# Attention scores of 64-channel heads: from two 128-row products per head to three 64-row products on the head's own half of the array

## The chip, the cores and the metric

The kernel runs on one core of one Trainium2 chip. A core has a matrix engine (TensorE, in the profile PE, with its loads of the stationary operand shown apart as PEld), a vector engine (VectorE, DVE), a scalar engine (ScalarE, ACT), a general engine (GpSimd, POOL) and a queue engine for transfers (SyncE, SP). Each engine takes its instructions in its own order and waits for the others by semaphores. The metric is the device time of one execution in microseconds (us).

A matrix product (MATMUL) multiplies a stationary operand, loaded beforehand by an LDWEIGHTS instruction, with a moving operand. Both lie in SBUF, with the contracted dimension along the 128 partitions, and the product is summed into a bank of PSUM. In a profile row `128*128 128x512` means 128 rows by 128 columns of stationary operand and a moving operand of 128 partitions by 512 elements.

## The reference

A two-layer encoder trunk on 512 tokens of 1024 channels, in float32. Layer 0 has an mLSTM mixer, layer 1 a banded attention; both have an attention to 256 memory tokens beside it, an output projection and a gated MLP with a causal convolution. What matters here are the two attentions with heads of 64 channels:

```python
def one_chunk(c):                      # band attention: 12 heads of 64 channels
    ...
    s = jnp.einsum('bqhd,bkhd->bhqk', qc, kc).astype(jnp.float32) * scale + bias
    s = jnp.where(valid, s, -jnp.inf)
    p = jax.nn.softmax(s, axis=-1).astype(vc.dtype)
    return jnp.einsum('bhqk,bkhd->bqhd', p, vc)

def memory_attention(q, mem, w_kv):    # 4 heads of 64 channels, in each of the two layers
    ...
    s = jnp.einsum('bshd,bmhd->bhsm', q, mk).astype(jnp.float32) * (MEM_HEAD_DIM ** -0.5)
    p = jax.nn.softmax(s, axis=-1).astype(mv.dtype)
    return jnp.einsum('bhsm,bmhd->bshd', p, mv).reshape(bsz, seq, MEM_WIDTH)
```

## The kernel before

All large products are done in a rounded float32 format (fp32r) with an operand cut in two: a high part, which is the value rounded to that format, and a low part, which is the rest. A product of two such numbers is summed from three products: high by high, high by low, low by high; the low by low term is left out. `mm3` (lines 194 to 196) issues these three for the projections, and nearly all rows of L194, L195 and L196 in the profile are such products.

Channels lie along the partitions, so a tile of 128 partitions holds a pair of heads: head 0 in partitions 0 to 63, head 1 in 64 to 127 (`HEADS`). For the scores of one head the kernel before uses the whole height of the array. `head_keys` makes for each head a tile whose own half holds the high part of the keys and whose other half holds their low part. `head_queries` makes two tiles for each head: one with the high part of the queries in both halves, one with the low part in the head's own half and zeros in the other (the zeros are a GpSimd memset, the copy into the other half an ACT instruction). `head_scores` (L600) then needs two products of 128 rows per head: the first gives high by high plus high by low, the second low by high. The four products of a pair stand head by head: both of head 0, then both of head 1.

Where these stand:

- `band_attention(j, ...)`, for six pairs j: `softmax(T)`, for four token tiles T of 128 tokens, calls `scores` with keys 0 to 128(T+1), so the moving operand is 128, 256, 384 and 512 wide. These are 24 calls. Six calls of `project_pair` make keys and queries.
- `memory_attention`, twice in each layer: four token tiles each against 256 memory tokens, 16 calls with a moving operand 256 wide. Four calls of `queries` and two of `load_memory_kv` make its operands.
- `mlstm_head` also calls `head_scores` (four heads, four tiles), and `qk_tile` calls `head_queries` and `head_keys` for it.

The order of the instructions on each engine comes from the order in which the program is written, which is woven: `weave` takes some steps of a filler (the projections of the next pair, or the output projection) for each step of the attention job, in the ratio that stands at the call, so that TensorE has products of the filler to do while the softmax of the attention runs on VectorE and ScalarE. A scheduler of the framework may move an instruction past others where its inputs come late; three PSUM banks (`psc`) are turned over by the scores, three by the projections (`pmm`), two by transposes and sums (`ptr`). The tiles of queries and keys come from a pool of 50 buffers of 128 x 512 (`u`).

Of the kernel before, what the change touches and what calls it, by code (L numbers as in the profile page):

```python
# [10 lines left out]
F32R = mybir.dt.float32r  # L11
I32 = mybir.dt.int32
AF = mybir.ActivationFunctionType
ALU = mybir.AluOpType
AX = mybir.AxisListType

P = 128
D = 1024
S = 512
# [7 lines left out]
HD = 64  # L27
# [22 lines left out]
def f(ap):  # L50
    return ap.bitcast(F32)
# [3 lines left out]
def trunk(  # L55
# [18 lines left out]
    nc = tc.nc  # L74
    V, A, G = nc.vector, nc.scalar, nc.gpsimd
# [14 lines left out]
    def sb(tag, shape, dtype=F32):  # L90
        count[0] += 1
        return pool.tile(shape, dtype, tag=tag, name=f"{tag}{count[0]}", bufs=bufs[tag])

    def ps(tag):
        count[0] += 1
        return psum.tile([P, S], F32, tag=tag, name=f"p{tag}{count[0]}", bufs=pbufs[tag])
# [38 lines left out]
    HEADS = (slice(0, HD), slice(HD, P))  # L135
# [3 lines left out]
    def split(hi, lo, src, on_act=True, pinned=False):  # L139
        high = A.copy(hi, src) if on_act else V.tensor_copy(hi, src)  # L140
        low = V.tensor_tensor(out=lo, in0=src, in1=f(hi), op=ALU.subtract)  # L141
        if pinned:
            pin(high)
            pin(low)
# [53 lines left out]
    def project(w, c0, act, tag="mm"):  # L198


        n = len(act)
        wh, wl = weights(rows(w, c0, P), n, P)
        o = ps(tag)
        for k in range(n):
            mm3(o, wh[:, k, :], wl[:, k, :], act[k][0], act[k][1], k == 0, k == n - 1)
            yield
        return o
# [250 lines left out]
    def value_weights(hf, u):  # L458
        n = AW // 2
        ex = rows(a_w_in, 4 * AW, 2 * AH, 2 * u, 2 * u + 2) if hf else None  # L460
        return load(rows(a_w_in, 2 * AW + hf * n, n, 2 * u, 2 * u + 2), 2, n, ex)

    with tc.manual_schedule(engines={mybir.EngineType.PE, mybir.EngineType.Activation, mybir.EngineType.DVE}):
# [56 lines left out]
        for q in range(KT // 2):  # L520
            k = 2 * q
# [39 lines left out]
        raw = value_weights(1, 0)  # L561
# [15 lines left out]
    def head_queries(t, scale=1.0):  # L577
        qs, ls = ([sb("u", [P, S], F32R) for _ in range(2)] for _ in range(2))
        for h, r in enumerate(HEADS):
            G.memset(f(ls[h])[HEADS[1 - h], :], 0.0)  # L580
            A.activation(qs[h][r, :], t[r, :], AF.Copy, scale=scale)
            V.scalar_tensor_tensor(ls[h][r, :], t[r, :], scale, f(qs[h])[r, :], op0=ALU.mult, op1=ALU.subtract)
        for h, r in enumerate(HEADS):
            A.copy(qs[h][HEADS[1 - h], :], f(qs[h])[r, :])
        return qs, ls

    def head_keys(t):
        ks = [sb("u", [P, S], F32R) for _ in range(2)]
        for h, r in enumerate(HEADS):
            A.copy(ks[h][r, :], t[r, :])  # L590
            V.tensor_tensor(out=ks[h][HEADS[1 - h], :], in0=t[r, :], in1=f(ks[h])[r, :], op=ALU.subtract)
        return ks

    def head_scores(o, h, q, tsl, k, c, first, keys_first=False):

        for i, part in enumerate(q):
            a, b = part[h][:, tsl], k[h][:, c]
            if keys_first:
                a, b = b, a
            nc.tensor.matmul(o, a, b, start=first and i == 0, stop=i == 1)  # L600

    def load_memory_kv(l):
        raw = sb("wr", [P, D])
        nc.sync.dma_start(raw, spill[l])
        k = head_keys(raw[:, :S])
        vs = []
        for m in range(2):
            v = sb("u", [P, S], F32R).rearrange("p (h c) -> p h c", h=4)
            src = raw[:, S + m * MEM : S + (m + 1) * MEM].rearrange("p (h c) -> p h c", h=4)
            split(v[:, :, :HD], v[:, :, HD:], src)  # L610
            vs.append(v)
        return k, vs
# [12 lines left out]
    def queries(o, row):  # L625

        if row is None:
            return head_queries(o, HD**-0.5)
        q = sb("t", [P, S])
        V.scalar_tensor_tensor(q, o, HD**-0.5, row, op0=ALU.mult, op1=ALU.mult)  # L630
        return head_queries(q)

    def scores(outs, q, tsl, k, c):

        for h in range(2):
            head_scores(outs[h], h, q, tsl, k, c, True)

    def memory_attention(q, kv, hp, mixes):

# [443 lines left out]
    e, u, c, r = (cpool.tile([P, TT, AH], F32, name=f"gate{i}") for i in range(4))  # L1083
# [131 lines left out]
    def mlstm_head(h):  # L1215
# [6 lines left out]
        def weighted_scores(s):  # L1222
            n = S - s * P
            sl = slice(s * P, (s + 1) * P)
            e = sb("t", [P, S])
            A.activation(e[:, :n], spreads.pop((h, s)), AF.Exp, bias=acol[:, s, h : h + 1])
            spread_exponents(order.index((h, s)) + NEXT)
            G.affine_select(
                out=e[:, :P], in_=e[:, :P], pattern=[[1, P]], base=0, channel_multiplier=-1,
                compare_op=ALU.is_ge, fill=0.0,  # L1230
            )
            yield
            o = ps("sc")
            kf, qf = ks[full], qs[full]
            mm3(o[:, :n], kf[0][:, sl], kf[1][:, sl], qf[0][:, s * P :], qf[1][:, s * P :], True, False)
            head_scores(o[:, :n], odd, qs[sh], slice(s * P, S), ks[sh], sl, False, True)
            V.scalar_tensor_tensor(e[:, :n], o[:, :n], DH**-0.5, e[:, :n], op0=ALU.mult, op1=ALU.mult)
            split(pt[:, RO[s] : RO[s + 1]], pt[:, 1280 + RO[s] : 1280 + RO[s + 1]], e[:, :n])
            yield
# [56 lines left out]
    run(fill)  # L1296
    fill = chain(a_tiles(2), a_memory_queries(0), a_tiles(3, 4), a_tiles(5), a_memory_queries(1))
    memkv = load_memory_kv(0)
    weave(mlstm_head(0), fill, 1.4)
    until(lambda: og[2] is not None, fill)  # L1300
# [38 lines left out]
    for j in range(KT):  # L1339
        wh, wl = weights(rows(ffn_w_down[0], j * P, P, FT - LAST, FT), LAST, P)  # L1340
        o = ps("mm")
# [23 lines left out]
    def project_pair(j):  # L1365
        def times_row(o):
            t = sb("t", [P, S])
            V.tensor_tensor(out=t, in0=o, in1=norm.row, op=ALU.mult)
            return t

        ov = yield from project(w_kv, AW + j * P, kvact)
        t = times_row(ov) if norm.row is not None else None
        o = yield from project(w_kv, j * P, kvact)
        if t is None:
            t = times_row(ov)
        k = head_keys(times_row(o))
        tp = ps("mm")
        for T in range(TT):
            nc.tensor.transpose(tp[:, T * P : (T + 1) * P], t[:, T * P : (T + 1) * P], ident)
        v = []  # L1380
        for i in range(2):

            w = sb("u" if j == 5 else ("fh", "fl")[i], [P, S], F32R).rearrange("p (h c) -> p h c", h=4)
            split(w[:, :, :HD], w[:, :, HD:], tp[:, i * MEM : (i + 1) * MEM].rearrange("p (h c) -> p h c", h=4))
            v += [w[:, :2, :], w[:, 2:, :]]
        q = queries((yield from project(b_w_in, j * P, act)), norm.row)
        qkv[j] = q, k, v
# [132 lines left out]
    for hf in range(2):  # L1520
# [6 lines left out]
        for Ts, pieces in groups:  # L1527
            for c in pieces:
                if c.start:
                    os_[Ts[0]] = ps("mm")  # L1530
                for u in range(n):
# [4 lines left out]
                    for T in Ts:  # L1536
                        for i in range(2):
                            k = 2 * u + i
# [58 lines left out]
```

## Time and profile before

| What | Value |
|---|---|
| median of 3 runs | 1179.24 us (1179.14 to 1179.31) |
| profiled execution, its own time | 1178.82 us |
| span of the profiled execution, first to last instruction | 1177.1 us |
| granted TensorE clock, mean | 0.999 |
| PE busy | 1167.3 us, 7005 products |
| DVE busy | 940.8 us |
| ACT busy | 728.9 us |
| POOL busy | 129.2 us |
| products of L600 (all score products of 64-channel heads, the mLSTM's 32 with them) | 192, busy 39.7 us together |

The busy time of PE counts the union of what its matmuls are shown to last, and these overlap: a 512-wide product is shown to last 0.39 us, while the next one starts 0.23 us after it. What a product costs on PE is therefore read from the distance between starts, in the view of instructions in order of time. The numbers after the bar in a group's row are busy us and mean ns of one; after the second bar stands the idle time of the engine just before them and what ended it.

### The profile page before, as it was taken

How to read it: one execution, taken by the hardware profiler on the slowest of the kernel's cores; microseconds unless marked ns; L12 is line 12 of the kernel's file. 1: busy time of each engine (PE TensorE's matmuls, PEld its weight loads, DVE VectorE, ACT ScalarE, POOL GpSimd, SP SyncE). 2: the span in 40 equal slices, each digit the busy share in tenths (PEclk: the TensorE clock that was granted, in tenths of full speed). 3: DMA queues.
4: the chain of work that ended last, by engine and by line, in shares of the span. 5: the costliest groups of instructions: out<-in, count | busy, mean ns of one | idle time of the engine just before them, and what ended most of it. 6: DMA issues, size and time to landing. Idle time of an engine off the chain costs nothing.

```text
span 1177.1 us, 18647 instructions
## 1 busy us (share of the span) xinstructions
PE 1167.3 (99%) x7005; PEld 1032.8 (88%) x7005; DVE 940.8 (80%) x1680; ACT 728.9 (62%) x1297; POOL 129.2 (11%) x222
## 2 busy tenths in 40 slices
PE   9999999999999999999999999999999999999997
PEld 9988888888889999999888888778889999999986
DVE  6777788887979878877688888897897887777755
ACT  6548677655656655666666677676565665666545
POOL 1111101010021121111020000101001011110100
PEclk9999999999999999999999999999999999999999
DMA  8645325243366766665563313325426466666551
GB/s 285 222 112 141 85 55 152 76 144 116 90 161 158 181 167 163 163 145 125 155 205 114 90 54 96 105 90 179 141 90 153 108 137 143 142 144 144 126 161 72
DMA packets 199420, 158.64 MB, mean 135 GB/s; under 512 B 8376, under 2 KB 178334, under 8 KB 199330
## 3 DMA queue, kind: packets, MB, share of 16 engines
q1 hardware_dynamic: 183170, 119.87, 34.6%
q0 software_dynamic: 15584, 36.67, 15.7%
q8 instruction: 55, 0.90, 0.3%
q10 hardware_dynamic: 576, 0.92, 0.2%
q14 instruction: 35, 0.29, 0.1%
HBM read 128.89 MB, written 32.46 MB: 137 GB/s over the span
## 4 chain that ended last, share of the span: by engine, by line
PE 95%; ACT 2%; DVE 2%; issue 0%; POOL 0%; POOLq 0%; DVEq 0%; ACTq 0%
PE pmm L194 18%; PE pmm L195 18%; PE pmm L196 18%; PE ptr L195 6%; PE ptr L194 6%; PE ptr L196 6%; PE psc L196 5%; PE psc L195 5%; PE psc L194 5%; PE psc L600 2%; PE ptr L1421 1%; PE ptr L1442 1%; PE ptr L1443 1%; PE ptr L669 0%; PE pmm L491 0%; PE pmm L470 0%
## 5 line engine op out<-in xcount | busy, mean ns | idle before, releaser
L194 PE MATMUL pmm<-u,wh 128*128 128x512 f32 (+1 forms) x968 | 333.2, 345 | 0.3 <-ACT u L140 0.3
L196 PE MATMUL pmm<-u,wl 128*128 128x512 f32 (+1 forms) x968 | 330.6, 342 | 0.0
L195 PE MATMUL pmm<-u,wh 128*128 128x512 f32 (+1 forms) x968 | 330.4, 341 | 0.0
L141 DVE TENSOR_TENSOR wl<-wr,wh 128x1024 fp32r<-128x1024 f32 (+3 forms) x172 | 199.7, 1162 | 83.0 <-ACT wh L140 81.5
L140 ACT CAST wh<-wr 128x1024 fp32r<-128x1024 f32 (+3 forms) x172 | 171.8, 1001 | 91.8 <-PE pmm L195 40.8
L196 PEld LDWEIGHTS pmm<-u,wl 128*128 128x128 f32 x968 | 181.8, 188 | 20.7
L194 PEld LDWEIGHTS pmm<-u,wh 128*128 128x128 f32 x968 | 181.8, 188 | 18.7 <-ACT u L140 1.2
L195 PEld LDWEIGHTS pmm<-u,wh 128*128 128x128 f32 x968 | 182.0, 188 | 18.1 <-DVE u L141 0.5
L194 PE MATMUL ptr<-u,wh 128*128 128x512 f32 x272 | 106.4, 391 | 0.0
L195 PE MATMUL ptr<-u,wh 128*128 128x512 f32 x272 | 106.2, 390 | 0.0
L196 PE MATMUL ptr<-u,wl 128*128 128x512 f32 x272 | 105.8, 389 | 0.0
L834 POOL DMA_DIRECT2D xspill<-t x64 | 55.5, 868 | 428.8 <-ACT t L833 416.3
L890 ACT COPY t<-pmm 128x256 f32<-128x256 f32 x102 | 38.2, 374 | 76.7 <-PE pmm L196 76.5
L141 DVE TENSOR_TENSOR u<-t,u 128x512 fp32r<-128x512 f32 (+1 forms) x94 | 54.0, 595 | 35.3 <-ACT u L140 35.3
L194 PE MATMUL pmm<-u,fh 128*128 128x256 f32 x272 | 75.4, 277 | 0.0
L194 PE MATMUL psc<-u,wh 128*128 128x256 f32 (+1 forms) x232 | 75.3, 324 | 0.0
L195 PE MATMUL pmm<-u,fh 128*128 128x256 f32 x272 | 75.2, 276 | 0.0
L196 PE MATMUL pmm<-u,fl 128*128 128x256 f32 x272 | 75.1, 276 | 0.0
L196 PE MATMUL psc<-u,wl 128*128 128x256 f32 (+1 forms) x232 | 75.1, 324 | 0.0
L195 PE MATMUL psc<-u,wh 128*128 128x256 f32 (+1 forms) x232 | 74.9, 323 | 0.0
L141 DVE TENSOR_TENSOR fl<-pt,fh 128x512 fp32r<-128x512 f32 x102 | 70.2, 689 | 5.1 <-ACT fh L140 1.4
L140 ACT CAST fh<-pt 128x512 fp32r<-128x512 f32 x102 | 62.8, 616 | 8.3 <-DVE pt L944 4.9
(352 smaller groups left out, 2494.6 us busy)
## 6 DMA issues: line engine op xcount, KB each, us to landing
wr<-in_ffn_w_up_dram SPq DMA_DIRECT2D x54, 512.0 KB, 6.3
wr<-in_ffn_w_down_dram SPq DMA_DIRECT2D x38, 512.0 KB, 5.4
pt<-in_ffn_w_up_dram SPq DMA_DIRECT2D x34, 512.0 KB, 8.2
xspill<-t POOLq DMA_DIRECT2D x64, 256.0 KB, 4.3
wr<-in_a_w_in_dram SPq DMA_DIRECT2D x20, 512.0 KB, 3.9
wr<-in_w_kv_dram SPq DMA_DIRECT2D x12, 512.0 KB, 4.1
xspill<-fh POOLq DMA_DIRECT2D x16, 256.0 KB, 2.6
xspill<-fl POOLq DMA_DIRECT2D x16, 256.0 KB, 2.9
```

The lines of the kernel that those rows point to most:

```text
L140: high = A.copy(hi, src) if on_act else V.tensor_copy(hi, src)
L141: low = V.tensor_tensor(out=lo, in0=src, in1=f(hi), op=ALU.subtract)
L194: nc.tensor.matmul(o, lh, rh, start=first, stop=False, skip_group_check=more)
L195: nc.tensor.matmul(o, lh, rl, start=False, stop=False, skip_group_check=more)
L196: nc.tensor.matmul(o, ll, rh, start=False, stop=last, skip_group_check=more)
L600: nc.tensor.matmul(o, a, b, start=first and i == 0, stop=i == 1)
L834: G.dma_start(xspill[j], t, accum_op=ALU.add)
L890: A.copy(o, r[:, :H])
L1421: nc.tensor.transpose(tp[:, b * P : (b + 1) * P], es[T, h][:, b * P : (b + 1) * P], ident)
L1442: nc.tensor.matmul(o2[:, s * P :], w, hi_at(pts[h], s, s, TT - s), start=s == 0, stop=False)
L1443: nc.tensor.matmul(o2[:, s * P :], w, lo_at(pts[h], s, s, TT - s), start=False, stop=s == TT - 1)
```

## The change

The keys and the queries of a pair are now one tile of high parts and one of low parts, 128 partitions each, with head 0 in the upper half and head 1 in the lower (`pair_parts`, one ACT and one DVE instruction). `scores` makes the three products of a head from the 64 rows of its own half, and goes through the two heads in turn: first product of head 0, first of head 1, second of head 0, and so on. Each of the two heads sums into its own PSUM bank, as before. In the built program these products carry a tile size of 64 rows by 128 columns and the position of row 0 or row 64. The mLSTM heads keep `head_queries`, `head_keys` and `head_scores`.

```diff
+    def pair_parts(t, scale=1.0):
+
+        hi, lo = (sb("u", [P, S], F32R) for _ in range(2))
+        A.activation(hi, t, AF.Copy, scale=scale)
+        V.scalar_tensor_tensor(lo, t, scale, f(hi), op0=ALU.mult, op1=ALU.subtract)
+        return hi, lo
+
...
     def load_memory_kv(l):
         raw = sb("wr", [P, D])
         nc.sync.dma_start(raw, spill[l])
-        k = head_keys(raw[:, :S])
+        k = pair_parts(raw[:, :S])
...
         if row is None:
-            return head_queries(o, HD**-0.5)
+            return pair_parts(o, HD**-0.5)
         q = sb("t", [P, S])
         V.scalar_tensor_tensor(q, o, HD**-0.5, row, op0=ALU.mult, op1=ALU.mult)
-        return head_queries(q)
+        return pair_parts(q)
 
     def scores(outs, q, tsl, k, c):
 
-        for h in range(2):
-            head_scores(outs[h], h, q, tsl, k, c, True)
+        for i, (a, b) in enumerate(((0, 0), (0, 1), (1, 0))):
+            for o, r in zip(outs, HEADS):
+                nc.tensor.matmul(o, q[a][r, tsl], k[b][r, c], start=i == 0, stop=i == 2)
...
-        k = head_keys(times_row(o))
+        k = pair_parts(times_row(o))
```

In TensorE's order, the second token tile of the first band pair: `psc` are the two score banks, the two names behind the arrow the moving operand (keys) and the stationary one (queries), `pmm` a projection of the filler. Before:

```order
L196 MATMUL pmm1248_6850<-u1192_6614,wl11247_6847 128x512
L600 MATMUL psc1261_6895<-u1231_6782,u1241_6832 128x256
L600 MATMUL psc1261_6895<-u1231_6782,u1243_6834 128x256
L600 MATMUL psc1262_6896<-u1232_6783,u1242_6833 128x256
L600 MATMUL psc1262_6896<-u1232_6783,u1244_6835 128x256
L194 MATMUL pmm1248_6850<-u1201_6652,wh11246_6846 128x512
```

Now:

```order
L196 MATMUL pmm1242_6838<-u1188_6612,wl11241_6835 128x512
L644 MATMUL psc1255_6885<-u1227_6780,u1237_6828 128x256
L644 MATMUL psc1256_6886<-u1227_6780,u1237_6828 128x256
L644 MATMUL psc1255_6885<-u1228_6781,u1237_6828 128x256
L644 MATMUL psc1256_6886<-u1228_6781,u1237_6828 128x256
L644 MATMUL psc1255_6885<-u1227_6780,u1238_6829 128x256
L644 MATMUL psc1256_6886<-u1227_6780,u1238_6829 128x256
L194 MATMUL pmm1242_6838<-u1197_6650,wh11240_6834 128x512
```

Six products stand where four stood, the two banks in turn, between the same 128-row products of the filler. Over the whole program the 240 products of L644 stand in 46 such unbroken runs: 27 of the band attention and 19 of the memory attention.

In TensorE's order, a place in the first memory attention where the two heads do not stand together (`psc353` before and `psc351` now is the bank of head 0 alone). Before:

```order
L196 MATMUL pmm342_1805<-u141_707,wl0341_1802 128x512
L600 MATMUL psc353_1860<-u236_1276,u305_1622 128x256
L600 MATMUL psc353_1860<-u236_1276,u307_1624 128x256
L194 MATMUL pmm363_1890<-u109_555,wh1361_1886 128x512
L195 MATMUL pmm363_1890<-u110_556,wh1361_1886 128x512
```

Now:

```order
L196 MATMUL pmm340_1795<-u141_707,wl0339_1792 128x512
L644 MATMUL psc351_1854<-u236_1276,u305_1620 128x256
L644 MATMUL psc351_1854<-u237_1277,u305_1620 128x256
L644 MATMUL psc351_1854<-u236_1276,u306_1621 128x256
L194 MATMUL pmm361_1886<-u109_555,wh1359_1882 128x512
L195 MATMUL pmm361_1886<-u110_556,wh1359_1882 128x512
```

Here three products of one half stand where two stood, with none of the other half between them.

In ACT's order, keys and queries of the first band pair before its first softmax (L1410 before, L1418 now). Before:

```order
L590 CAST u1231_6782<-t1230_6780 64x512
L590 CAST u1232_6783<-t1230_6780 64x512
L140 CAST fl1235_6796<-pmm1233_6788 128x4x64
L140 CAST wh01305_7059<-wr1304_7057 128x1024
L581 ACTIVATE u1241_6832<-t1240_6830 64x512
L581 ACTIVATE u1242_6833<-t1240_6830 64x512
L584 CAST u1241_6832<-u1241_6832 64x512
L584 CAST u1242_6833<-u1242_6833 64x512
L1410 ACTIVATE t1255_6878,s21257_6880<-t1255_6878,s21256_6879 128x128
```

Now:

```order
L597 ACTIVATE u1227_6780<-t1226_6778 128x512
L140 CAST fl1231_6792<-pmm1229_6784 128x4x64
L140 CAST wh01299_7053<-wr1298_7051 128x1024
L597 ACTIVATE u1237_6828<-t1236_6826 128x512
L1418 ACTIVATE t1249_6868,s21251_6870<-t1249_6868,s21250_6869 128x128
```

Six instructions of 64 partitions became two of 128. Over the program ACT has 38 instructions fewer, DVE 18, POOL 20 (all of them memsets), and on SP one load of output weights stands five loads later than before.

## The prediction

> **What bounds the kernel now.** I began with the page's busy times and the chain that ended last.
>
> ```profile
> PE 1167.3 (99%) x7005; PEld 1032.8 (88%) x7005; DVE 940.8 (80%) x1680; ACT 728.9 (62%) x1297; POOL 129.2 (11%) x222
> PE 95%; ACT 2%; DVE 2%; issue 0%; POOL 0%; POOLq 0%; DVEq 0%; ACTq 0%
> ```
>
> TensorE is busy 99% of the span and carries 95% of the chain. Since such shares hide stages, I next took the busy time of each engine in the two stretches in which the changed scores lie (100 to 235 us: memory attention of layer 0 beside mLSTM; 630 to 800 us: band and memory attention of layer 1), and what TensorE waited for.
>
> ```profile
> 100.00:235.00 135.00, 134.69 (x688) 113.54 (x687) 107.21 (x217) 95.15 (x167) 14.55 (x32) 1.00 0.38 103
> 630.00:800.00 170.00, 168.88 (x879) 139.25 (x879) 147.95 (x379) 119.14 (x281) 11.83 (x22) 1.00 0.30 91
> ```
>
> The columns are PE, PEld, DVE, ACT and POOL busy, then the granted clock. In both stretches PE is idle for 0.31 + 1.12 = 1.4 us in all, with DVE at 79% and 87%. So these stretches are as long as TensorE's own work, and the question is what that work becomes; what ACT and DVE save there can return about 1.4 us.
>
> **What the scores cost on TensorE now.** The view in order of time, of PE alone, at the four token tiles of the first band pair:
>
> ```profile
> 632.08 0.39 PE L196 MATMUL pmm<-u,wl 128*128 128x512 f32 x1
> 632.31 0.64 PE L600 MATMUL psc<-u,u 128*128 128x128 f32 x4
> 632.79 0.45 PE L194 MATMUL pmm<-u,wh 128*128 128x512 f32 x1
> 633.07 0.39 PE L195 MATMUL pmm<-u,wh 128*128 128x512 f32 x1
> 633.30 0.39 PE L196 MATMUL pmm<-u,wl 128*128 128x512 f32 x1
> 633.53 0.64 PE L600 MATMUL psc<-u,u 128*128 128x256 f32 x4
> 634.00 0.40 PE L194 MATMUL pmm<-u,wh 128*128 128x512 f32 x1
> ...
> 637.00 0.88 PE L600 MATMUL psc<-u,u 128*128 128x384 f32 x4
> 637.72 0.39 PE L194 MATMUL pmm<-u,wh 128*128 128x512 f32 x1
> ...
> 640.24 1.07 PE L600 MATMUL psc<-u,u 128*128 128x512 f32 x4
> 641.15 0.39 PE L194 MATMUL pmm<-u,wh 128*128 128x512 f32 x1
> ```
>
> From start to start the four products take 0.48, 0.47, 0.72 and 0.91 us. The narrowest delays its successor too (633.07 - 632.79 = 0.28 where 0.23 is usual), so 0.53. One product thus costs 0.115 (256 wide), 0.175 (384) or 0.23 (512); the 128-wide ones take 0.12 though they are half as wide as the 256-wide, since they wait for their weight loads (below). A pair costs 0.53 + 0.47 + 0.72 + 0.91 = 2.63 us, six pairs 15.8. The 64 products of the memory attentions are 256 wide; at 0.12 each they cost 7.7 us. Together 23.5 us, which the change replaces.
>
> **The price of changing the array's shape.** No product of 64 rows stands in this trace. The nearest is a group of eight transposes from 4 rows (L1167 and L1168; the built program gives them a tile of 32 rows by 128 columns). First PE, then the weight loads (PEld), of one place:
>
> ```profile
> 86.13 0.39 PE L196 MATMUL pmm<-u,wl 128*128 128x512 f32 x1
> 86.45 0.22 PE L1167 MATMUL ptr<-ident,t 4*128 4x4 f32 x1
> 86.53 0.20 PE L1168 MATMUL ptr<-ident,t 4*128 4x4 f32 x1
> ...
> 86.90 0.20 PE L1168 MATMUL ptr<-ident,t 4*128 4x4 f32 x1
> 87.03 0.50 PE L194 MATMUL pmm<-u,wh 128*128 128x512 f32 x1
> 87.37 0.39 PE L195 MATMUL pmm<-u,wh 128*128 128x512 f32 x1
> ```
>
> ```profile
> 85.91 0.19 PEld L196 LDWEIGHTS pmm<-u,wl 128*128 128x128 f32 x1
> 86.44 0.13 PEld L1167 LDWEIGHTS ptr<-ident,t 4*128 4x128 f32 x1 [0.35 <-issue]
> 86.50 0.14 PEld L1168 LDWEIGHTS ptr<-ident,t 4*128 4x128 f32 x1
> ...
> 86.87 0.14 PEld L1168 LDWEIGHTS ptr<-ident,t 4*128 4x128 f32 x1
> 87.03 0.19 PEld L194 LDWEIGHTS pmm<-u,wh 128*128 128x128 f32 x1
> 87.14 0.19 PEld L195 LDWEIGHTS pmm<-u,wh 128*128 128x128 f32 x1
> ```
>
> Elsewhere a load starts as soon as the product before it has started and is hidden under it (L196's at 85.91, for the product at 86.13). Here the first small load waits until 86.44, though the next slot was due at 86.13 + 0.23 = 86.36, and no semaphore is named (the idle 0.35 is put down to "issue"). On the way back the load of L194 waits until 87.03, 0.13 after the last small product started, and its product can only run 0.11 later, when the load is done: the load behind it starts at 87.14 and L195 runs 0.23 after that. So going in costs 0.09 plus an uncovered first load, and coming out 0.13 + 0.11 = 0.24 after the last product has streamed.
>
> The Trainium skill, "TensorEngine Tiling (Array Packing)", section Key Properties, says that a change of the tiling mode, and not of the tile alone, drains TensorE. These rows agree for tiles of fewer rows. The trace also disagrees for tiles of fewer columns, where nothing waits:
>
> ```profile
> 58.90 0.34 PE L196 MATMUL pmm<-wh,u 128*128 128x384 f32 x1
> 59.08 0.27 PE L1119 MATMUL ptr<-ident,lf 128*4 128x128 f32 x1
> ```
>
> The 384-wide slot of 0.175 ends at 59.08, when the 4-column transpose (built with 32 columns) starts. By the rule the change would pay the price at each run; were 64-row tiles like these column tiles, it would not, which is the second rival.
>
> **What the change adds on TensorE.** 240 products (6 in place of 4 for each pair and token tile), in the 46 unbroken runs of the order, each with an entry and an exit: 0.09 + 0.13 + 0.11 = 0.33 us, plus the streaming of its last product (0.055, half of the 256-wide price, or 0.115, 0.175, 0.23), under which nothing is loaded any more.
>
> Inside a run two prices are open. The first is whether two halves stream side by side; the ends are yes (three widths per run) and no (six). I take yes, since the two sit on other rows and other banks; no row shows it. The skill's "TensorE: Matmul & The Clock Gate", section Part 3, says that products on different row groups start about 4 ns apart and overlap; no run here shows that. The second is the load. Full-height loads of this form follow each other at 0.11 (87.03, 87.14), the loads in the reduced shape at 0.06 (86.44, 86.50). One end is 0.11 each, one after the other, the other 0.055, as if two halves loaded together. The new loads share the data form with the first row and the reduced shape with the second, so I take the middle, 0.085.
>
> With that, a run of six: 128 wide 0.33 + 0.51 + 0.055 = 0.90; 256 wide 0.33 + 0.51 + 0.115 = 0.96; 384 wide 0.33 + 0.17 + 3 x 0.175 = 1.02; 512 wide 0.33 + 0.17 + 3 x 0.23 = 1.19. A pair 4.07 against 2.63, six pairs +8.6. The last pair's 128-wide run is cut into four, three more passages at 0.385: +1.2. Memory attention: 96 loads x 0.085 + 19 runs x (0.33 + 0.115) = 16.6 against 7.7: +8.9. Sum +18.7 us, all on the path, as nothing else sets the end there.
>
> **What it takes from the other engines.**
>
> ```profile
> L581 ACT ACTIVATE u<-t 64x512 fp32r<-64x512 f32 x20 | 12.6, 628 | 0.2
> L584 ACT CAST u<-u 64x512 fp32r<-64x512 f32 x24 | 14.9, 620 | 0.6
> L590 ACT CAST u<-t 64x512 fp32r<-64x512 f32 x16 | 9.9, 619 | 0.2
> L140 ACT CAST u<-t 128x512 fp32r<-128x512 f32 x62 | 38.4, 620 | 13.6 <-DVE t L783 8.1 <-DVE t L620 3.9 <-DVE t L1009 1.5
> L582 DVE SCALAR_TENSOR_TENSOR u<-t,u 64x512 fp32r<-64x512 f32 x20 | 13.7, 683 | 0.4
> L580 POOL MEMSET u<- 64x512 f32 x24 | 12.6, 524 | 137.9 <-PE psc L600 69.9 <-PE pmm L195 40.1 <-ACT t L1410 23.0
> ```
>
> 64 partitions cost ACT what 128 do (0.62). Ten calls for queries drop three ACT instructions each and eight for keys one: 38 x 0.62 = 23.6 us of ACT. DVE drops 18 x 0.69 = 12.4 us, POOL 20 x 0.52 = 10.4 us. Hardly any lies on the path: it returns between 0 and the 1.4 us of idle PE; I take 1. Fewer tiles in the pool and an output-weight load five places later on SP I cost at nothing: PE waits for neither buffers nor transfers there.
>
> Sum: 1178.8 (profiled) + 18.7 - 1 = 1196.5 us, say 1197; the profiled execution lies 0.4 under the median of 1179.24, which changes nothing here.
>
> **Rivals.**
>
> *The halves stream in turn.* The alternation gives nothing. Runs cost (load 0.11 at first, then six widths, at least six loads) 1.05, 1.14, 1.49 and 1.82, a pair 5.50: +17.2, +1.2, memory 96 x 0.117 + 19 x 0.44 - 7.7 = +11.9. With -1 that is 1208. For it: the trace has no two products side by side. Against it: other rows, other banks.
>
> *No passage price, and side by side: faster.* If 64-row tiles follow 128-row products with their loads hidden, as the 4-column tile does, three widths replace four: with loads at 0.055 a pair falls to 0.33 + 0.35 + 0.53 + 0.69 = 1.90, -4.4, memory 48 x 0.117 - 7.7 = -2.1; with -1 that is 1171. With loads at 0.085 it is 1176, with 0.11 1181. It decides below 0.06 us for entry and exit of a run together (a gain of 2.9 over 46 runs, at loads of 0.085), where I reckon with 0.33 and the last streaming. Against it: the rows at 86.44 and 87.03.
>
> *The products pass as ordinary whole-array products.* Then no passage and six in turn at 0.11 or their width: 3.79 a pair, +7.0, memory 11.2 - 7.7 = +3.5, less 1: 1188.
>
> **How the numbers follow.** Likeliest: passages paid, halves side by side, loads from 0.055 to 0.11: chance 0.57. Its ends are 1191 (loads 0.055: pairs +5.8, +1.2, memory +6.3, -1) and 1202 (0.11: +11.6, +1.2, +11.3, -1). In turn 1208: 0.17. No passage price: 0.14, of which 0.10 faster, 0.03 the same, 0.01 slower. Whole-array products 1188: 0.07. The remaining 0.05, for disturbed order or waits for two banks at once, splits into 0.01 faster, 0.01 the same, 0.03 slower. Same means within 0.2%, 2.4 us, about what a measurement can tell. So faster 0.11, same 0.04, slower 0.85. The range of 8 in 10 leaves out the cases without a passage price and a tail above: 1184 to 1209.
>
> **What would show it.** Right: the first load of an L644 run starts some 0.1 us after the slot before it ended, the load behind the run 0.13 after its last stream; inside, starts of the two halves lie closer than a width; PE's time in the two stretches grows by 19 us while ACT's and DVE's falls. Wrong: loads of L644 hidden under the projection before them, or starts of the halves a full width apart, or PE newly idle before L644 on a bank.

## The result, and the profile after

The changed kernel takes 1189.49 us (median of 4 runs, 1189.32 to 1189.66) against 1179.28 us for the kernel before (1179.14 to 1179.93). The ratio is 1.0089, 95% interval 1.0076 to 1.0101: slower by 10.2 us. The profiled execution took 1189.59 us, its span is 1187.9 us (before 1177.1), at the same granted clock of 0.999.

The page of the kernel after, busy times and the chain that ended last:

```profile
PE 1179.2 (99%) x7085; PEld 1029.3 (87%) x7085; DVE 928.9 (78%) x1662; ACT 703.7 (59%) x1259; POOL 120.2 (10%) x202
PE 93%; issue 4%; DVE 1%; ACT 1%; POOL 0%; POOLq 0%; ACTq 0%; DVEq 0%
```

TensorE has 80 products more and is busy 11.9 us longer; ACT lost 25.2 us, DVE 11.9 and POOL 9.0. TensorE still sets the end. New in the chain is "issue" with 4%: time in which the engine waited for nothing that the profile shows. It is not the price of the change: one piece of 47.08 us, from 143.41 on, makes nearly all of it. There the chain is followed back along GpSimd, and TensorE is busy through the whole stretch (columns as below):

```profile
143.41:190.49 47.08, 47.08 (x235) 37.71 (x234) 36.61 (x71) 34.67 (x57) 0.00 (x0) 1.00 0.34 107
```

The two stretches of the scores, kernel after (length, then PE, PEld, DVE, ACT and POOL busy, then the granted clock, as before):

```profile
100.00:235.00 135.00, 134.87 (x684) 110.51 (x683) 101.95 (x208) 88.63 (x156) 13.58 (x27) 1.00 0.37 97
630.00:800.00 170.00, 169.68 (x904) 130.94 (x903) 131.80 (x343) 93.88 (x237) 5.46 (x10) 1.00 0.29 87
```

PE is idle for 0.13 + 0.32 = 0.45 us, where it was 1.4 us: no new idle time has come up, while ACT and DVE have much more room. (The stretches are the same pieces of the clock, not the same work: the second ends earlier in the program now.)

The second token tile of the first band pair, kernel after. The view in order of time, PE alone, taken three times: at the first two products of the run, at its last two, and for the whole run (a row groups the products that lie in the window asked for).

```profile
637.71 0.40 PE L196 MATMUL pmm<-u,wl 128*128 128x512 f32 x1
638.04 0.39 PE L644 MATMUL psc<-u,u 64*128 64x256 f32 x2
...
638.38 0.28 PE L644 MATMUL psc<-u,u 64*128 64x256 f32 x2
...
638.04 0.62 PE L644 MATMUL psc<-u,u 64*128 64x256 f32 x6
638.60 0.50 PE L194 MATMUL pmm<-u,wh 128*128 128x512 f32 x1
638.93 0.39 PE L195 MATMUL pmm<-u,wh 128*128 128x512 f32 x1
```

The weight loads at the same place:

```profile
637.49 0.19 PEld L196 LDWEIGHTS pmm<-u,wl 128*128 128x128 f32 x1
638.04 0.18 PEld L644 LDWEIGHTS psc<-u,u 64*128 64x128 f32 x2 [0.36 <-issue]
...
638.59 0.19 PEld L194 LDWEIGHTS pmm<-u,wh 128*128 128x128 f32 x1
638.70 0.19 PEld L195 LDWEIGHTS pmm<-u,wh 128*128 128x128 f32 x1
```

Read in order: the slot of L196 ends at 637.71 + 0.23 = 637.94; the first load of 64 rows starts 0.10 later, where a load otherwise runs under the product ahead of it. Two products then last 0.39 us together, which is what one lasts (0.38): in the trace their starts lie 3 to 4 ns apart. The loads of the next pair start 0.107 us after the first two loads. The products of the next pair start 0.22 us after the first two (0.107 for the uncovered loads, 0.115 for the streaming), those of the third 0.12 after that, the last at 638.39. The load of L194 waits until 638.59, 0.09 after that one has streamed (638.39 + 0.115 = 638.50), and is not covered: L195 starts 0.23 after the load behind it.

To compare whole runs I take the time from the end of the slot ahead of a run to the start of the second product behind it, and subtract the slot of the first product behind it. The entry and the uncovered load at the exit are then in it: here 638.93 - 0.23 - 637.94 = 0.76 us. By that measure an undisturbed run of six costs 0.68, 0.76, 0.92 and 1.10 us (128, 256, 384 and 512 wide), where four products in the first pair before had cost 0.53, 0.47, 0.72 and 0.91 (the 0.53 holds a delay of 0.09, told of in the section on why). All 240 products of L644 cost 38.1 us; the 160 they replace cost 26.5 (all 192 of L600 cost 32.2, of which the mLSTM's 32 are 5.7 in the kernel after, where they still stand apart). So TensorE pays 11.6 us more in the scores, and the span grew by 10.8.

What PE waited for, kernel after (us in all, times, longest):

```profile
PE pmm L470 <- DVE mcf L127: 1.1, 1, 1.1
PE ptr L677 <- DVE t L668: 0.2, 1, 0.2
PE pmm L194 <- ACT u L140: 0.2, 1, 0.2
```

This is the whole list. PE stands idle ahead of no score product.

What is left of the preparation on ACT and DVE (kernel after, groups by line and form):

```profile
L597 ACT ACTIVATE u<-t 128x512 fp32r<-128x512 f32 x14 | 8.9, 634 | 0.0
L598 DVE SCALAR_TENSOR_TENSOR u<-t,u 128x512 fp32r<-128x512 f32 x14 | 9.6, 683 | 0.0
```

An instruction on 128 partitions takes what one on 64 took (634 and 683 ns now, 628 and 683 before), and does both heads.

### The profile page after: what moved, and what is told of

Read it like the earlier page. It is cut to its first block, busy times and chain, and to the rows that moved or that the text cites. A ratio compares the mean times of both kernels' runs of the same rounds, so it can differ in the third digit from the quotient of the medians.

```text
span 1187.9 us, 18713 instructions
## 1 busy us (share of the span) xinstructions
PE 1179.2 (99%) x7085; PEld 1029.3 (87%) x7085; DVE 928.9 (78%) x1662; ACT 703.7 (59%) x1259; POOL 120.2 (10%) x202
## 4 chain that ended last, share of the span: by engine, by line
PE 93%; issue 4%; DVE 1%; ACT 1%; POOL 0%; POOLq 0%; ACTq 0%; DVEq 0%
PE pmm L194 18%; PE pmm L195 17%; PE pmm L196 17%; PE ptr L195 6%; PE ptr L194 6%; PE ptr L196 6%; PE psc L196 5%; PE psc L195 5%; PE psc L194 5%; PE psc L644 2%; PE ptr L1429 1%; PE ptr L1451 1%; PE ptr L1450 1%; PE ptr L691 1%; PE pmm L491 0%
## 5 line engine op out<-in xcount | busy, mean ns | idle before, releaser
L194 PE MATMUL pmm<-u,wh 128*128 128x512 f32 (+1 forms) x968 | 336.8, 348 | 0.3 <-ACT u L140 0.2
L195 PE MATMUL pmm<-u,wh 128*128 128x512 f32 (+1 forms) x968 | 330.2, 341 | 0.0
L196 PE MATMUL pmm<-u,wl 128*128 128x512 f32 (+1 forms) x968 | 329.8, 341 | 0.0
L194 PEld LDWEIGHTS pmm<-u,wh 128*128 128x128 f32 x968 | 181.6, 188 | 24.4 <-issue 2.7
L196 PEld LDWEIGHTS pmm<-u,wl 128*128 128x128 f32 x968 | 181.7, 188 | 21.6
L195 PEld LDWEIGHTS pmm<-u,wh 128*128 128x128 f32 x968 | 182.0, 188 | 18.3 <-DVE u L141 0.5
L194 PE MATMUL ptr<-u,wh 128*128 128x512 f32 x272 | 106.4, 391 | 0.0
L195 PE MATMUL ptr<-u,wh 128*128 128x512 f32 x272 | 106.2, 391 | 0.0
L196 PE MATMUL ptr<-u,wl 128*128 128x512 f32 x272 | 105.8, 389 | 0.0
L194 PE MATMUL pmm<-u,fh 128*128 128x256 f32 x272 | 75.4, 277 | 0.0
L194 PE MATMUL psc<-u,wh 128*128 128x256 f32 (+1 forms) x232 | 75.2, 324 | 0.0
L195 PE MATMUL pmm<-u,fh 128*128 128x256 f32 x272 | 75.2, 276 | 0.0
L196 PE MATMUL pmm<-u,fl 128*128 128x256 f32 x272 | 75.1, 276 | 0.0
L196 PE MATMUL psc<-u,wl 128*128 128x256 f32 (+1 forms) x232 | 75.1, 324 | 0.0
L195 PE MATMUL psc<-u,wh 128*128 128x256 f32 (+1 forms) x232 | 75.0, 323 | 0.0
```

What stands on the lines that cost most here:

```text
L194: nc.tensor.matmul(o, lh, rh, start=first, stop=False, skip_group_check=more)
L195: nc.tensor.matmul(o, lh, rl, start=False, stop=False, skip_group_check=more)
L196: nc.tensor.matmul(o, ll, rh, start=False, stop=last, skip_group_check=more)
```

## Experiments

The change does three things: it shortens the preparation, it makes six products of four, and it puts them on halves of the array in turn. The kernels below take these apart one by one. Each is compared with runs of the kernel before on its own chip: 1179.18 us for the two kernels of whole height, the exchanged loops and the half-height product in the kernel before, 1178.62 us for the other three. Where a kernel's scores are not the reference's, it serves for the timing alone.

### The short preparation alone

The kernel after, with four products of 128 rows for a pair; from the new tiles, so the scores are not the reference's:

```diff
-        for i, (a, b) in enumerate(((0, 0), (0, 1), (1, 0))):
-            for o, r in zip(outs, HEADS):
-                nc.tensor.matmul(o, q[a][r, tsl], k[b][r, c], start=i == 0, stop=i == 2)
+        for o in outs:
+            for i, (a, b) in enumerate(((0, 0), (1, 0))):
+                nc.tensor.matmul(o, q[a][:, tsl], k[b][:, c], start=i == 0, stop=i == 1)
```

> The kernel after, with four products of 128 rows for a pair in place of six of 64 rows, made from the new tiles (so the two heads' scores are summed together and one of the three terms is left out; the time of the products is that of the kernel before). TensorE's work is that of before, ScalarE, VectorE and GpSimd have the savings of the change. Theory that TensorE's own work alone sets the end: 1177.9 to 1179.3 us, since only the 1.4 us that PE stood idle can come back. Rival, that the savings on ScalarE and VectorE are worth more than PE's idle time shows (late operands hidden in overlapping ends): 1174 to 1177 us.

Measured: 1177.09 us (1176.39 to 1177.32), ratio 0.9983 (0.9974 to 0.9991): 2.1 us faster than before. That lies between what the two theories gave, and it is more than the 1.4 us of idle PE that I had taken as the most that could return. Where it comes from shows in the narrowest tile of the third band pair, before:

```profile
682.05 0.79 PE L600 MATMUL psc<-u,u 128*128 128x128 f32 x4
682.68 0.45 PE L196 MATMUL pmm<-u,wl 128*128 128x512 f32 x1
```

and in this kernel:

```profile
681.34 0.56 PE L644 MATMUL psc<-u,u 128*128 128x128 f32 x4
681.73 0.45 PE L194 MATMUL pmm<-u,wh 128*128 128x512 f32 x1
```

The same four products take 0.63 us from start to start before, and 0.39 here. In the run the trace of before has 0.28 us from the third start to the fourth (0.11 here), but no idle PE, for each product is shown to last longer than its slot. So PE's idle time is no bound on what PE loses to waits. The 160 score products cost 24.7 us here and 26.5 before: 1.8 of the 2.1 us. Before, the load queue also has separate semaphore instructions ahead of some of these products (the view of line L600):

```profile
L600 PEldq EVENT_SEMAPHORE  x20: 51/51/51, 215.9 to 768.9; - x20
```

In this kernel L644 has two of them. Some stand inside the runs that are late (one starts at 682.44, ahead of the fourth product above); whether the delay is that instruction or the operand that it waits for, is not separated.

### Six products, whole height

The kernel after, with its six products of the pair made from all 128 rows. The order on every engine is that of the kernel after; the scores mix the two heads.

```diff
-            for o, r in zip(outs, HEADS):
-                nc.tensor.matmul(o, q[a][r, tsl], k[b][r, c], start=i == 0, stop=i == 2)
+            for o in outs:
+                nc.tensor.matmul(o, q[a][:, tsl], k[b][:, c], start=i == 0, stop=i == 2)
```

> The kernel after, with its six products of a pair made over all 128 rows, the two banks in turn (the two heads' scores are summed together). The array keeps its shape, so there are no passages, and the products run one after the other. Passage theory: a pair costs 0.66 + 0.70 + 1.05 + 1.38 = 3.79 us instead of 2.63, six pairs +7.0, memory attention 96 x 0.117 - 7.7 = +3.5, less up to 1: 1188.8 us. Rival, that the 80 added products and loads as such are the loss of the kernel after: the same time as that kernel, 1189.5 us. The two lie close here; the run gives the price of an added whole-array product, which the next ones need.

Measured: 1187.54 us (1187.14 to 1188.69), ratio 1.0071 (1.0056 to 1.0087). Against the four whole products, 80 added ones cost 10.5 us, 0.13 each, about the price read off the trace of before (0.12 for the 256-wide ones that are most of them). The two theories lay too close together for this run to decide between them. Without any halves the same work is thus slower than before by 8.4 us, and 2 us faster than with them: the halves as the change uses them bring nothing in sum, as their passages cost more than they save.

### Six products, one half

The kernel after, with both heads read from rows 0 to 63, so head 1 gets the scores of head 0. The order is again that of the kernel after, the shape of the products too; only the position of every second product differs.

```diff
-            for o, r in zip(outs, HEADS):
+            for o, r in zip(outs, (HEADS[0], HEADS[0])):
```

> The kernel after, with both heads' products made from rows 0 to 63 (head 1 gets head 0's scores). The same instructions in the same order, the same 46 passages, but the two heads cannot stream or load side by side. Theory that the halves' overlap is what holds the loss of the kernel after down: each side-by-side pair of its trace costs one width more (0.11 for 128, 0.117 for 256, 0.175 for 384, 0.23 for 512 wide): band attention 6 x 3 x (0.11 + 0.117 + 0.175 + 0.23) = 11.4, memory attention about 29 pairs x 0.117 = 3.4, so 1204 us. Rival, that the overlap is only in the shown starts and the products take their turns anyway: 1189.5 us.

Measured: 1202.82 us (1202.51 to 1203.29), ratio 1.0204 (1.0189 to 1.0219), as the theory of the halves side by side had it. PE in order of time at the second token tile of the first band pair, first up to the start of the second product, then whole:

```profile
639.50 0.40 PE L196 MATMUL pmm<-u,wl 128*128 128x512 f32 x1
639.83 0.50 PE L644 MATMUL psc<-u,u 64*128 64x256 f32 x2
...
639.83 0.98 PE L644 MATMUL psc<-u,u 64*128 64x256 f32 x6
640.74 0.50 PE L194 MATMUL pmm<-u,wh 128*128 128x512 f32 x1
641.08 0.40 PE L195 MATMUL pmm<-u,wh 128*128 128x512 f32 x1
```

Two products last 0.50 here, 0.39 in the kernel after: one starts a width behind the other. The run costs 1.11 where it cost 0.76 on two halves and 0.72 at whole height. In the 512-wide tile it is 1.80 to 1.10. So side by side is real, and worth 13.3 us between the two medians, or 14.0 with each against its own kernel before.

Against the six products at whole height, which also run in turn, the one-half kernel is slower by 15.8 us (+24.2 less +8.4, each against its own kernel before). The two differ by 46 passages, so one passage into the 64-row shape and back costs 0.34 us.

### Head 0 whole, then head 1

The kernel after with the two loops exchanged, meant to put the halves one after the other:

```diff
-        for i, (a, b) in enumerate(((0, 0), (0, 1), (1, 0))):
-            for o, r in zip(outs, HEADS):
+        for o, r in zip(outs, HEADS):
+            for i, (a, b) in enumerate(((0, 0), (0, 1), (1, 0))):
```

> The kernel after, with the three products of head 0 first and then the three of head 1. Same products, same loads, 43 passages instead of 46; only the last of head 0 and the first of head 1 can stream side by side. Passage theory with halves side by side: 43 x 0.41 = 17.6 us for passages, products 5 widths instead of 4: a pair 0.55 + 0.59 + 0.88 + 1.15 = 3.17 against 2.63, six pairs +3.2, memory +1.7, less 1: 1201 us; without any overlap between the heads 1206. Rival, that added products and loads as such are the loss: 1189.5 us, as the kernel after.

Measured: 1191.55 us (1191.18 to 1191.76), ratio 1.0106 (1.0092 to 1.0120). This missed what either theory gave. PE up to 638.23, then the whole run:

```profile
637.88 0.40 PE L196 MATMUL pmm<-u,wl 128*128 128x512 f32 x1
638.21 0.40 PE L644 MATMUL psc<-u,u 64*128 64x256 f32 x2
...
638.21 0.63 PE L644 MATMUL psc<-u,u 64*128 64x256 f32 x6
638.77 0.50 PE L194 MATMUL pmm<-u,wh 128*128 128x512 f32 x1
```

Within 20 ns of the first product a second has started (10 ns behind it in the trace), and both last 0.40 together. In the program the second product is of the same half as the first, and in the kernel above two of one half last 0.50. So the one that has started must be the other half's first, which the program has in fourth place: each half takes its products as if from a queue of its own. The semaphore updates in the trace show the same. In the built program the third and the sixth product of this run update a semaphore, and in the narrowest tile of the first pair the first, second, third and sixth; in the trace it is the fifth and the sixth to start, and in the narrowest tile the first, third, fifth and sixth. Both fit the two halves taken in turn, and not the order of the program. The run costs 0.77, as in the kernel after. The exchange changes nothing of what it was meant to change, and it could not tell the theories apart; the one-half kernel did.

The 2.1 us that it is slower than the kernel after do not come from the score runs (all 240 products cost 36.9 us here, 38.1 in the kernel after). The list of what PE waited for has, in this kernel, first:

```profile
PE ptr L1429 <- DVE pt L141: 1.9, 6, 0.5
```

This wait is not in the list of the kernel after. Why it comes with the exchange, and what makes up the rest, no run here shows.

### The price of a passage, without any other change

The kernel before, in which only the last of the four products of a pair (head 1, low queries) uses the 64 rows of its own half. The other half of that operand holds zeros, so the scores are the same, with as many products as before, of the same width, and 40 passages.

```diff
         for h in range(2):
-            head_scores(outs[h], h, q, tsl, k, c, True)
+            for i, part in enumerate(q):
+                r = HEADS[1] if h == 1 and i == 1 else slice(0, P)
+                nc.tensor.matmul(outs[h], part[h][r, tsl], k[h][r, c], start=i == 0, stop=i == 1)
```

> The kernel before, where only the last of the four products of each call, low queries of head 1 by its keys, is made from the 64 rows of its own half (the other half of its queries is zeros, so the scores are the same). Not one product or load more than before, but 40 passages from whole array to half and back. Passage theory: 40 x 0.41 = +16.4 us, 1195.7 us. Rival, that added products and loads are the loss: 1179.3 us. Rival, that a passage costs only where loads of several halves stand: under 1185 us.

Measured: 1190.65 us (1190.54 to 1191.29), ratio 1.0100 (1.0086 to 1.0114): 11.5 us for 40 passages, 0.29 each. The second token tile of the first band pair, PE over the whole run (the row has the form of its first product), then the fourth product alone and on:

```profile
637.00 0.40 PE L196 MATMUL pmm<-u,wl 128*128 128x512 f32 x1
637.23 0.83 PE L638 MATMUL psc<-u,u 128*128 128x256 f32 x4
...
637.68 0.38 PE L638 MATMUL psc<-u,u 64*128 64x256 f32 x1
637.99 0.50 PE L194 MATMUL pmm<-u,wh 128*128 128x512 f32 x1
638.33 0.39 PE L195 MATMUL pmm<-u,wh 128*128 128x512 f32 x1
```

The run costs 0.87 where it cost 0.47. Half the rows, the same columns, and 0.40 us more: the price lies on the change of shape, whichever product brings it. The passage that I had named is therefore a cause, and the theory without it (no change of time) is out. 40 times 0.40 would be 16 us, though, and the whole of the score runs grew by 13.4 (the 128-wide run at the start of the first pair grew from 0.53 to 0.79 only). The rest of the gap to 11.5 is not settled; waits that the kernel before has in these runs could have hidden some passages, but no run here shows that.

### Fewer passages

The kernel after, with runs put together: in the memory attention the scores of two token tiles stand one behind the other, and in the band attention those of T = 0 and T = 1, which share two banks. That makes 35 runs of 46, with the same 240 products.

```diff
                 scores([s[:, i, :] for s in ss], q, slice(T * P, (T + 1) * P), k, slice(hp * MEM, (hp + 1) * MEM))
-                yield
+            yield
+            yield
...
-        yield from softmax(0)
-        yield from softmax(1)
+        banks = [ps("sc") for _ in range(2)]
+        s0, s1 = score_tile(0, banks, 0), score_tile(1, banks, P)
+        yield from softmax(0, s0)
+        yield from softmax(1, s1)
```

> The kernel after, same products on the same halves, with fewer passages: in the memory attention the scores of two token tiles stand one behind the other (the two steps of filler that stood between and behind them come after both), and in the band attention the first two token tiles share two banks and stand one behind the other. 35 unbroken runs of 64-row products instead of 46. Passage theory, with 0.38 to 0.41 us for each: 11 x 0.4 = 4.4 us less than the kernel after, 1185.1 us (1184 to 1187 with what the other order of the softmax does). Rival, that products and loads as such are the loss: 1189.5 us.

Measured: 1186.45 us (1186.40 to 1186.70), ratio 1.0065 (1.0049 to 1.0082): 3.0 us under the kernel after, 2.4 with each against its own kernel before; 0.22 to 0.28 for each run saved, and within the 1184 to 1187 that the passage theory gave. T = 0 and T = 1 of the first band pair, in order of time (the row of twelve has the form of its first products; the last six are 256 wide):

```profile
635.33 0.39 PE L196 MATMUL pmm<-u,wl 128*128 128x512 f32 x1
635.65 0.96 PE L644 MATMUL psc<-u,u 64*128 64x128 f32 x12
636.54 0.50 PE L194 MATMUL pmm<-u,wh 128*128 128x512 f32 x1
636.88 0.39 PE L195 MATMUL pmm<-u,wh 128*128 128x512 f32 x1
```

Twelve products cost 1.08 (in the kernel after 0.68 + 0.76 = 1.44). The kernel before needs 0.53 + 0.47 = 1.00 for the eight that they replace (0.91 without the delay in the 0.53), so even this run does not pay.

### Less preparation in the kernel before

The short preparation was worth 2.1 us, so I tried to have some of it without the halves: the kernel before, with its 24 copies of the queries into the other half made by GpSimd and not by ACT.

```diff
-            A.copy(qs[h][HEADS[1 - h], :], f(qs[h])[r, :])
+            G.tensor_copy(qs[h][HEADS[1 - h], :], f(qs[h])[r, :])
```

> The kernel before, with the copies of the high queries into the other half made by GpSimd instead of ScalarE (24 of 64 partitions by 512, 14.9 us of ACT). TensorE's products are those of before. If the 2.1 us that four whole products with the short preparation gained come from the load on ScalarE, a part of them comes without any 64-row product: 1177.5 to 1178.8 us. Rival, that the copies come later from GpSimd and TensorE waits for the queries: 1180 to 1183 us.

Measured: 1195.52 us (1194.10 to 1198.43), ratio 1.0145 (1.0128 to 1.0162), slower than both kernels and outside what either theory gave. First in the list of what PE waited for:

```profile
PE psc L600 <- DVE s L1406: 8.0, 5, 2.7
```

A copy takes 0.93 us there (0.62 on ACT), and the two of a pair stand in turn. But the longest waits come from what stands behind the copies. GpSimd also issues the transfers of the bias (L1396) that the first instruction of the softmax (L1406) adds to the scores. First GpSimd, then VectorE:

```profile
633.61 2.15 POOL L584 CAST u<-u 64x512 fp32r<-64x512 f32 x2 [16.07 <-ACT u L581]
635.72 1.09 POOL L1396 DMA_DIRECT2D bias<-rep  x2
...
640.01 0.29 DVE L1406 CUSTOM_DVE_ANT_0 t<-psc,bias 128x128 f32<-128x128 f32 x1 [3.70 <-DMA bias<-rep]
```

GpSimd waits for the queries before it can copy, and the two transfers go out behind the copies at 635.72; in the kernel before they go out at 614.45, 18 us ahead of the softmax. So VectorE waits for the bias (16.4 us in 8 places, in the kernel before not once), and the score banks that it empties come free late: that is the "s L1406" that PE waits for. The run therefore does not show what the load on ACT is worth. The place in order of time, PE alone:

```profile
637.74 0.40 PE L195 MATMUL pmm<-u,wh 128*128 128x512 f32 x1
640.36 0.50 PE L600 MATMUL psc<-u,u 128*128 128x256 f32 x2 [2.22 <-DVE s L1406]
...
641.25 0.63 PE L195 MATMUL pmm<-u,wh 128*128 128x512 f32 x1
641.68 0.63 PE L196 MATMUL pmm<-u,wl 128*128 128x512 f32 x1
642.11 0.63 PE L194 MATMUL pmm<-u,wh 128*128 128x512 f32 x1
```

After a stall of 2.22 us the products follow each other at 0.43 and not at 0.23. The stretch behind it:

```profile
640.40:644.00 3.60, 3.60 (x12) 2.79 (x13) 2.52 (x13) 3.01 (x10) 0.00 (x0) 0.59 0.02 7
```

The granted clock is 0.59 there. So a wait of TensorE can cost more than its own length, though not each does: of the three stalls of over 2 us in this trace, those of 2.22 and 2.65 us were followed by a clock of 0.50 for 3.4 us, the one of 2.10 us by the full clock. And the clock is the smaller part of the loss: the profiled execution took 1198.43 us at a mean clock of 0.996, while two of the four took 1194.1 and 1194.2 us at 0.999, 15.5 us more than the kernel before. No kernel that computes the reference's scores came out faster than the kernel before.

### The ladder

| Kernel | Against before, us | What the step adds |
|---|---|---|
| four products, whole height, short preparation | -2.1 | the preparation that falls away |
| six products, whole height | +8.4 | +10.5: 80 products at 0.13 |
| six products, one half | +24.2 | +15.8: 46 passages at 0.34 |
| six products, two halves (the change) | +10.2 | -14.0: halves side by side |

## Why the prediction was right, and where its sum was off

The sign and the mechanism were right: slower, since the passages (15.8 us) cost more than the products side by side save (the 14.0 of the halves less the 10.5 of the added products, 3.5 us) and the preparation returns (2.1 us). The size was not: a loss of 17.7 us was forecast, and it is 10.2. Forecast 1197 us, measured 1189.5, within the range (1184 to 1209) but 1.5 us under the low end of the likeliest case's own (1191 to 1202). Point by point:

| Step of the prediction | Forecast | Measured |
|---|---|---|
| entry of a run | 0.09 and an uncovered load | 0.10 and an uncovered load |
| exit, after the last product has streamed | 0.13 + 0.11 | 0.09 + 0.11 |
| the two halves | side by side | side by side, 3 to 4 ns apart |
| a load inside a run | 0.085 (0.055 to 0.11) | 0.107 for two, so 0.055 |
| run of six, 128 / 256 / 384 / 512 wide | 0.90 / 0.96 / 1.02 / 1.19 | 0.68 / 0.76 / 0.92 / 1.10 |
| all 240 products | 23.5 + 18.7 = 42.2 | 38.1 |
| the 160 products before | 23.5 | 26.5 (24.7 without the long preparation) |
| what ACT, DVE and POOL return | 1 (0 to 1.4) | 2.1 |

**The bound** was right: TensorE stayed at 99%, and of the 46 us that ACT, DVE and POOL lost, 2.1 came back (by the kernel with four whole products). That fewer tiles and the later weight load cost nothing was right too, as the list of waits shows.

**The passage** was right in place and size. The rows of eight small transposes of few rows, the nearest case in the trace of before, gave 0.33 us and the last product's streaming; the runs show 0.10 + 0.09 + 0.11 and that streaming. The kernel before with one half-height product shows it by itself. The Trainium skill, "TensorEngine Tiling (Array Packing)", section Key Properties, has the rule that a change of the tiling mode drains TensorE; the gap from 637.94 to 638.04 agrees with it for tiles of 64 rows.

**The load inside a run** is the term that was mis-sized most. "I take the middle, 0.085": no row could decide between 0.055 and 0.11, and it was the low end, because the loads of two halves run side by side as the products do. For the 128-wide and 256-wide tiles that is 0.51 - 0.32 = 0.19 us per run; with the exit shorter by 0.04 it explains both rows of the table to within 0.03. The wide tiles, whose loads are hidden but for the first pair, came out 0.10 lower by the same two corrections (0.17 to 0.107, 0.13 to 0.09).

**Memory attention** hid some of that error. Band attention cost 22.2 us against a forecast of 6 x 4.07 + 1.2 = 25.6. Memory attention cost 15.8 against 16.6, though at the cheaper load it should have been 96 x 0.055 + 19 x 0.445 = 13.7. I had reckoned all its products as pairs. The trace has only some 29 of 48 possible pairs side by side, for where the order puts three or six products of one head together (the second place that the change's section shows) there is nothing to run beside them. At one such run, kernel after, PE alone, up to 223.78 and whole:

```profile
223.55 0.50 PE L644 MATMUL psc<-u,u 64*128 64x256 f32 x2
...
223.55 0.97 PE L644 MATMUL psc<-u,u 64*128 64x256 f32 x6
224.45 0.50 PE L195 MATMUL pmm<-u,wh 128*128 128x512 f32 x1
```

Two products last 0.50, as in the one-half kernel, and the run costs 1.10 where a paired one costs 0.76. The order on the engines had shown such places; the sum did not use them.

**What the scores cost before** was too low by 3.0 us. I multiplied one pair's clean runs by six, and took PE's idle time as all that waits could cost. About a dozen runs of the kernel before are later than the clean ones, with PE shown busy. Even the pair that I took as clean has such a run, its narrowest: one of the semaphore instructions of L600 starts at 632.55, between the third and the fourth load, and the fourth product starts 0.175 us after the third. In the kernel with the short preparation, without that instruction, the distance is 0.11 and the run costs 0.44. So the 0.53 that the prediction put down to weight loads is 0.44 for the loads and 0.09 for that delay. So the step "it returns between 0 and the 1.4 us of idle PE" had a wrong upper bound, and the short preparation alone returns 2.1.

Together: 42.2 - 38.1 = 4.1 us on the side of the new products and 26.5 - 23.5 = 3.0 on that of the old ones. These 7.1 us are the distance from the forecast 17.7 (18.7 - 1) to the growth of the span of 10.8, to 0.2 us.

**The rivals.** "In turn" (1208) is ruled out by the kernel that does run in turn: its run prices of 1.00, 1.11, 1.44 and 1.80 are near what this rival was given (1.05, 1.14, 1.49, 1.82), and the kernel after does not have them, except in unpaired runs. "No passage price" (faster) is ruled out by the half-height product in the kernel before. "Whole-array products" gave 1188, near the measured time, but by another way: that kernel, run above, takes 1187.5, and it shows neither the gap ahead of the first load nor the halves side by side. Only the rows tell it from the change, not the time, and that its time lies near the measured one is chance: passages and side-by-side halves nearly cancel (15.8 against 14.0).

**The signs named beforehand** held, but in size: first load 0.10 after the slot, starts of the halves closer than a width, no PE newly idle ahead of L644 on a bank; PE's growth was 11.6 us in the scores and not 19, and the load behind the run waits 0.09 and not 0.13. The Trainium skill, "TensorE: Matmul & The Clock Gate", section Part 3, has products on different row groups start about 4 ns apart; the 3 to 4 ns of the kernel after agree.

## What to carry to other kernels

Splitting a product over halves of the array pays only if the run in that shape is long: here each run paid 0.34 us for the passage (0.10 + 0.107 + 0.09 + 0.11 = 0.41 in the run shown), and six products side by side saved 0.12 us of streaming for 256 columns (three widths instead of four). From these numbers I estimate that three to four token tiles of 256 columns would have to stand in one run only to come out even. With one tile the change loses 0.29 us (0.76 against 0.47); the run at 744.81 of the kernel after, which holds two, still loses 0.15 (1.10 against 0.95 for eight such products at 769.51 before). The two halves must also stand in one run of the engine's order at each place, not only together in the source (in turn they need not be: three of one ahead of three of the other ran side by side too); and the idle time of a busy engine is no upper bound on its waits where the profile shows each instruction longer than its slot, so compare distances between starts over all runs, not over one clean place.

## What the runs showed of the hardware that I had not expected

- The halves of the array take products as if from queues of their own: with three products of head 0 ahead of three of head 1 in the program, the first of head 1 started 10 ns after the first of head 0.
- The loads of two halves run side by side as well: 0.107 us for a pair, where loads of whole height follow each other at 0.11.
- At 256 columns a change of shape costs about the same for one product as for six: one product of 64 rows among products of 128 added 0.40 us to a run with nothing added to compute, six in turn cost 0.39 more than six of whole height (1.11 against 0.72).
- A stall of 2.2 us on TensorE was followed by 3.6 us at a granted clock of 0.59, with products of 512 columns 0.43 apart and not 0.23; another of 2.1 us in the same trace was not.
